# Two-layer hybrid encoder in split fp32: the grouped queries' product moved ahead of the keys' and values', with a separate inverse square root for the keys

## The chip, the cores and the metric

The kernel runs on one core of one Trainium2 chip, as one program. The metric is the device time of one execution in microseconds (us). A core has a matmul engine (PE), whose weight loads (PEld) overlap its matmuls, and three engines for elementwise work: DVE, ACT and POOL. SP issues the DMAs. Matmuls write to PSUM, in banks of 128 partitions x 512 fp32 values; everything else lives in SBUF.

## The reference, cut to what matters

Input x is 512 tokens by 1024 channels in fp32. There are two layers. Each runs three branches over the same normalized input, merges them with gates, and ends with a gated MLP. The change touches the first product and the grouped-query branch.

```
h = rms_norm(x, attn_norm_g[l])
proj = h @ w_in[l]
c_q, c_kv, k_rope, gq, gk, gv, pool_in, gate_logits = split_columns(proj, IN_SIZES)
                 # 256,  128, 32, 512, 128, 128, 512, 3 x 1024 columns
def gqa_branch(q_raw, k_raw, v_raw, qn_g, kn_g, cos, sin):
    q = q_raw.reshape(b, s, GQA_HEADS, GQA_HEAD_DIM)       # 8 heads of 64
    k = k_raw.reshape(b, s, GQA_KV_HEADS, GQA_HEAD_DIM)    # 2 heads of 64
    v = v_raw.reshape(b, s, GQA_KV_HEADS, GQA_HEAD_DIM)
    q = apply_rope(rms_norm(q, qn_g), cos, sin)
    k = apply_rope(rms_norm(k, kn_g), cos, sin)
    o = block_attention(q, k, v)
o_mla  = mla_branch(c_q, c_kv, k_rope, ...)   # latents, own head norms and rope
o_pool = pool_branch(pool_in, ...)            # means over windows 2/4/8/16, minus the token
merged = sum over branches of sigmoid(gate) * (o_branch @ w_branch)
x = x + merged @ w_out[l]
x = x + (silu(u_gate) * u_val) @ ffn_w_down[l]   # u: conv of rms_norm(x) @ ffn_w_up
```

`rms_norm` divides by the root of the mean square over the last axis; for a head that is one number per token and head.

## The kernel before

**Split products.** Every fp32 operand of a matmul is held as a high and a low half (fp32r). A product (`mm3`) is three matmuls: high x high, high x low, low x high. The normalized input lies in `HH` and `HL`, channels on the partitions, in 8 chunks (`kc`). Its division by the root of the mean square (`rt`, or `rbc` spread over the partitions) is applied when a product is read out of PSUM.

**Weights.** All weights stream through SP's queue in the order in which they are used, into three buffers of up to 1024 columns (`raw`; the first eight pieces have buffers of their own). Two pieces before its use, a piece is split: ACT writes the high half `wh` (L209), then POOL, or DVE where a cost rule says so, the low half `wl` (L216). Each has four buffers. Lines L209 to L240 are those of a small wrapper class, `Engine`, which every operation of DVE, ACT and POOL goes through. So the profile names them by tile, and nearly all of an engine's work stands on a few lines.

**The order of the work.** It is not found at run time. The Python program that builds the kernel carries a model clock (`Clock`). Matmuls advance it. Elementwise work is put in as chains of steps: `chain(a, b, c)` puts `a` into a heap at its due time, and each next step is due when the model says that the one before is done. Steps come out in the order of their due times, and that is the order of the instructions on each engine; each engine then takes its instructions strictly in order. Steps of different chains interleave. Everything inside one step is issued without a break. `done(key)` and `need(key)` connect chains with the matmul stream, `at(t, fn)` puts in a single step at a time.

**PSUM.** Eight banks under five names: acc 2, S 1, ST 2, AV 2, mi 1. `ps(tag)` takes the next buffer of that name; on the chip its first matmul waits until the last reader of the buffer's former content is done.

**A layer's first part, in the order of PE.**

1. Latents (256 + 128 columns), token-major: 8 chunks x 4 token blocks x 3 matmuls, banks acc, acc, ST, ST. Then the sums for `rt` into S. On DVE `rsqrt_steps` computes an inverse square root in ten small operations: a first guess `y` from the bits (L228), then three rounds of three (`yt`, `yt`, `y`). Each of the ten is a step of its own, so others can come between. Then ACT copies the latents out (`lat_evac`, tile `mx`), their mean squares (`ssc`) go through the same ten steps, and `lat_norm` scales `mx` in eight DVE operations.
2. Four groups of pool channels, 8 x 3 matmuls each, banks AV, AV, mi, S. Each is read out by DVE (`pp`, times `rbc`), summed over its window in one to four additions (`win`), corrected at the edges and mixed (`mix`), and split (`mxh` on ACT, `mxl` on DVE).
3. Transposes of `mx` (L345), three banks: acc, acc, ST. They are split into `cth` (ACT) and `ctl` (DVE).
4. Keys, values and the rotary key of the latent branch, 288 columns, token-major, 96 matmuls, banks ST, AV, AV, mi. ACT copies each block out (`gkn`, values, `krt`), DVE forms the values' low halves, the sums of squares of the keys, and their rotary embedding in 16 operations (`gk_rope`).
5. Queries, 512 columns, 96 matmuls, banks acc, acc, ST, S; between chunks 3 and 4 the 12 matmuls of the pool product (`pool_product`), banks AV, AV, mi, ST. `gq_evac` copies each block out on ACT, its square's row sums are formed on DVE (`ssr`), and its rotary embedding runs on POOL and DVE (`gqr`).
6. One inverse square root for all 40 numbers per token block column, 32 of the queries and 8 of the keys (`rsqrt_steps(ssr, 40, ...)`), then the scaling of the keys (`gk`, done key `gkn`), then that of the four query blocks.
7. Gate products of the pool branch as a filler, `Filler`, in units of three matmuls: `PRE_A` = 13 units, and more while the planner's clock says that the keys are not ready. Then the keys' transposes, `gk_turn` (L345, bank mi, split into `ka` and `kb`), then the attention of the grouped queries, each step of it placed between filler units at a written position, then the latent branch in the same manner, whose heads use `rsqrt_steps` twice more (32 numbers each).

**The rotary tables** (`tables`, 12 DVE operations: constants times the head norms' gains, tiles `tabg`, `tabm`) come at planner time 28.0 in layer 0, and 8 us into layer 1.

Of the kernel before, what the change touches and what calls it, by code (L numbers as in the profile page):

```python
# [11 lines left out]
F32R = mybir.dt.float32r  # L12
I32 = mybir.dt.int32
# [60 lines left out]

def _widths():

    r = [384] * KC + [T] * 8 + [288] * KC + [T] * 4 + [T] + [T] * 4
    for br in (2, 1, 0):
        for k, _ in _order(br):
            r += WIDTHS[k]  # L80
    return r + [T] * (2 * KC) + [T] * (4 * FC) + [T] * (2 * FC)
# [36 lines left out]
class Clock:  # L118
# [37 lines left out]
    def done(self, *key):  # L156
        self.ready[key] = self.fin + self.SEM
# [86 lines left out]
def trunk(ctx: ExitStack, tc: tile.TileContext, x, w, prm, gb, cst, out):  # L244
# [41 lines left out]
    def f(ap):  # L286
        return ap.bitcast(F32)
# [118 lines left out]
    def rsqrt_steps(a, n, key):  # L406

        y = small("y0", [P, 64])[:, :n]
        t = small("yt", [P, 64])[:, :n]

        def newton(to):
            return [lambda: V.tensor_tensor(t, y, a, ALU.mult),
                    lambda: V.scalar_tensor_tensor(t, t, -0.5, y, ALU.mult, ALU.mult),
                    lambda: V.scalar_tensor_tensor(to, t, 1.5, y, ALU.add, ALU.mult)]

        return [lambda: V.tensor_scalar(y.bitcast(I32), a.bitcast(I32), -0.5, RSQRT_BITS, ALU.mult, ALU.add),
                *newton(y), *newton(y), *newton(a), lambda: done(*key)]

    def norm_finish(gen, sq, out):

# [45 lines left out]
    def rope_steps(dst, src, cs, sn, shape, half, eng2):  # L466

        hold = []

        def parts():  # L470
            t2 = slot("rp2")
            n = 1
            for s in shape[1:]:
                n *= s
            t2v = t2[:, :n].rearrange("p (a b) -> p a b", b=shape[-1])
            hold.append(t2v)
            eng2.tensor_tensor(t2v[:, :, 0:half], src[:, :, half:2 * half], sn[:, :, 0:half], ALU.mult)
            eng2.tensor_tensor(t2v[:, :, half:2 * half], src[:, :, 0:half], sn[:, :, half:2 * half], ALU.mult)
            if dst is not src:
                V.tensor_tensor(dst, src, cs, ALU.mult)  # L480

        def add():
            if dst is src:
                V.tensor_tensor(dst, src, cs, ALU.mult)
            V.tensor_tensor(dst, dst, hold[0], ALU.add)

        return [parts, add]

    def layer(l, sq, xsrc):
# [161 lines left out]
        kvb = [ps(t) for t in ktags]  # L651
        tok_major(kvb, 288)
        gkn, kj, gk1 = slot("gkn"), slot("kj"), slot("gk1")
        krt = small("krt", [P, 4, 32], bufs=1)
        VG = []
        for b in range(4):
            v = slot("vg", F32R)
            vh = v[:, 0:256].rearrange("p (h f) -> p h f", f=P)
            vl = v[:, 256:384].rearrange("p (h f) -> p h f", f=64)
            V.memset(f(vh[:, :, 64:P]), 1.0)  # L660
            VG.append((vh, vl))

        def kv_evac(b):
            vh, vl = VG[b]
            src = kvb[b][:, P:2 * P].rearrange("p (h f) -> p h f", f=64)
            A.activation(gkn[:, b * P:b * P + P], kvb[b][:, 0:P], AF.Copy, scale=rtok(b))
            A.activation(vh[:, :, 0:64], src, AF.Copy, scale=rtok(b))
            A.activation(krt[:, b, :], kvb[b][:, 2 * P:288], AF.Copy, scale=rtok(b))

            def lo():  # L670
                V.scalar_tensor_tensor(vl, src, rtok(b), f(vh[:, :, 0:64]), ALU.mult, ALU.subtract)
                free(ktags[b])
                done("vg", l, b)
            chain(lo, after=ck.fin - ck.now + 0.1)

        def gk_rope():
            for b in range(4):
                k = gkn[:, b * P:b * P + P].rearrange("p (h f) -> p h f", f=64)
                o = gk1[:, b * P:b * P + P].rearrange("p (h f) -> p h f", f=64)
                cs = bc(tabs[1][:, None, 64 * b:64 * b + 64], [P, 2, 64])  # L680
                sn = bc(tabs[1][:, None, 256 + 64 * b:320 + 64 * b], [P, 2, 64])
                for fn in rope_steps(o, k, cs, sn, [P, 2, 64], 32, V):
                    fn()

        def gk_sum():
            A.activation(kj[:, :T], gkn[:, :T], AF.Square)

        def gk_sum2():
            V.tensor_reduce(ssr[:, 32:40], kj[:, :T].rearrange("p (h f) -> p h f", f=64), AX.X, ALU.add)

        chain(*[lambda b=b: kv_evac(b) for b in range(4)], gk_sum, gk_sum2, gk_rope)

        opool = {}

        def pool_product():
            wh, wl = wnext()
            for g, tag in enumerate(("AV", "AV", "mi", "ST")):
                need(("mix", l, g))
                acc = ps(tag)
                ws = slice(g * P, g * P + P)  # L700
                mm3(acc, wh[:, ws], wl[:, ws], mixed[g][0][:, :T], mixed[g][1][:, :T], True, True)
                oh, ol = slot("oph", F32R), slot("opl", F32R)
                opool[g] = (oh, ol)
                chain(*split(oh[:, :T], ol[:, :T], acc, col(PRM_PS + g)),
                      lambda g=g, tag=tag: (free(tag), done("op", l, g)))


        qtags = ("acc", "acc", "ST", "S")
        gqb = [ps(t) for t in qtags]
        tok_major(gqb, T, pool_product)  # L710
        gqn = [slot("gq") for _ in range(4)]
        gqo = [slot("gqr") for _ in range(4)]

# [17 lines left out]
            chain(*rope_steps(o, q, cs, sn, [P, 8, 64], 32, G), lambda: done("gqr", l, b), after=dt - 0.4)  # L731

        def gq_mean():
            V.tensor_scalar(ssr, ssr, 1.0 / 64, EPS, ALU.mult, ALU.add)

        def gk_norm():
            o = gk1[:, :T].rearrange("p (h f) -> p h f", f=64)
            V.tensor_tensor(o, o, bc(ssr[:, 32:40].unsqueeze(2), [P, 8, 64]), ALU.mult)
            done("gkn", l)

        def gq_norm(b):
            o = gqo[b][:, :T].rearrange("p (h f) -> p h f", f=64)
# [1 line left out]
            done("gqn", l, b)  # L744

        chain(*[lambda b=b: gq_evac(b) for b in range(4)], ([("gqs", l, b) for b in range(4)], gq_mean),
              *rsqrt_steps(ssr, 40, ("ssr", l)), gk_norm,
              *[([("gqr", l, b)], lambda b=b: gq_norm(b)) for b in range(4)])

        KAB = []  # L750

# [637 lines left out]
def _pack_weights(i):  # L1389
    res = []  # L1390
    for l in range(L):
        cq, ckv, kr, gq, gk, gv, pool, gate = np.split(
            i["w_in"][l], np.cumsum([256, 128, 32, 512, 128, 128, 512]), axis=1)

        def rows(*parts):
            wm = np.concatenate(parts, axis=1)
            return [wm[kc * P:kc * P + P] for kc in range(KC)]

        res += rows(cq, ckv)
        for g in range(4):  # L1400
            res += _cut(_blocks(pool[:, g * P:g * P + P], KC))
        res += rows(gk, gv, kr)
        res += rows(gq)
# [103 lines left out]
```

## Time and profile before

| | |
|---|---|
| median of the runs | 1699.12 us (three runs, 1698.81 to 1700.99) |
| the profiled execution | 1701.64 us, of which the span of the core's instructions is 1699.4 |
| mean granted PE clock | 0.994 of full speed |
| busy share of the span | PE 97%, PEld 79%, POOL 57%, DVE 55%, ACT 46% |
| instructions in the span | 20370, of these PE 7360 matmuls, DVE 1502, ACT 1375, POOL 771 |
| DMA | 145.40 MB, 86 GB/s over the span |

The profile is that of one execution. Times in its views are in us from the start of the span; the chain of waits and the timeline name an instruction by engine, line (L341 is `mm`, L345 is `turn`), the tiles written and read (`out<-in`), and, in square brackets, how long the engine had stood idle before it and what released it. "<-DVE mx L228" says that an instruction of DVE on tile `mx`, line 228, ended that wait. A row of the timeline groups neighbours of the same form: the first number is its start, the second its length, x8 the count. A row of the windows view has, for a stretch of the span, its length, the busy time (and count) of PE, PEld, DVE, ACT and POOL, the granted PE clock, the DMA share, and the GB/s.

### The profile page before, as it was taken

What the parts mean: (1) busy time and instruction counts of PE and PEld (TensorE: products, weight loads), DVE (VectorE), ACT (ScalarE), POOL (GpSimd) and SP (SyncE); (2) the same over time, 40 slices, a digit from 0 to 9 for tenths busy, and PEclk for the clock granted to TensorE, in tenths of its full rate; (3) what the DMA queues carried; (4) which work ended last, traced back from release to release, by engine and by line L of the source; (5) the groups of instructions that cost most, each with busy time, mean ns of one, the idle gap of its engine ahead of it and who ended that gap; (6) DMA issues with size and microseconds to landing.
All of it is one profiled execution on the core that took longest, in us unless ns stands there. A gap on an engine that the chain in (4) does not pass through costs nothing.

```text
span 1699.4 us, 20370 instructions
## 1 busy us (share of the span) xinstructions
PE 1655.1 (97%) x7360; PEld 1335.7 (79%) x7360; DVE 938.3 (55%) x1502; ACT 782.6 (46%) x1375; POOL 972.3 (57%) x771
## 2 busy tenths in 40 slices
PE   8889999999999999999999899999999999999999
PEld 7767767778888888888888677777788888888887
DVE  6765976643356666630156759766433666666100
ACT  5356655653344444433234576556534444444221
POOL 4455565764566566655545565666645665666543
PEclk9999999999999999999999999999999999999999
DMA  5221112113423332333333211111233232232331
GB/s 176 85 72 44 56 48 62 38 62 112 124 87 89 98 100 87 100 106 116 100 101 95 70 44 47 61 49 38 75 118 118 87 100 92 94 94 93 111 118 56
DMA packets 44596, 145.40 MB, mean 86 GB/s; under 512 B 5072, under 2 KB 6352, under 8 KB 44496
## 3 DMA queue, kind: packets, MB, share of 16 engines
q1 hardware_dynamic: 44352, 144.10, 27.0%
q8 instruction: 58, 0.95, 0.2%
q14 instruction: 42, 0.34, 0.1%
q10 hardware_dynamic: 144, 0.01, 0.0%
HBM read 139.90 MB, written 4.19 MB: 85 GB/s over the span
## 4 chain that ended last, share of the span: by engine, by line
PE 87%; DVE 8%; issue 2%; ACT 1%; POOL 1%; DMA 0%; SPq 0%; POOLq 0%; DVEq 0%; ACTq 0%
PE ps_acc L341 40%; PE ps_ST L341 23%; PE ps_AV L341 20%; PE ps_S L341 2%; DVE gqr L216 1%; PE ps_mi L345 1%; DVE yt L216 1%; DVE nm L224 1%; POOL wl L216 1%; PE ps_mi L341 1%; DVE MQ L216 1%; DVE yt L220 0%; DVE win L216 0%; DVE y L220 0%; DVE y L228 0%
## 5 line engine op out<-in xcount | busy, mean ns | idle before, releaser
L216 POOL TENSOR_TENSOR wl<-raw,wh 128x512 fp32r<-128x512 f32 (+1 forms) x514 | 678.5, 1330 | 493.4 <-ACT wh L209 432.1
L209 ACT ACTIVATE wh<-raw 128x512 fp32r<-128x512 f32 (+3 forms) x522 | 313.8, 608 | 194.2 <-PE ps_ST L341 70.8
L220 DVE SCALAR_TENSOR_TENSOR a<-u,prm,a 128x512 f32<-128x512 f32 x176 | 239.6, 1362 | 79.2 <-ACT a L209 74.0
L341 PE MATMUL ps_acc<-HH,wh 128*128 128x512 f32 x624 | 247.1, 396 | 2.2 <-DVE XM L220 2.2
L341 PE MATMUL ps_acc<-HH,wl 128*128 128x512 f32 x624 | 246.7, 395 | 1.2 <-POOL wl L216 1.2
L341 PE MATMUL ps_acc<-HL,wh 128*128 128x512 f32 x624 | 246.2, 395 | 0.0
L216 POOL TENSOR_TENSOR pl<-pe,ph 128x512 fp32r<-128x512 f32 x105 | 138.9, 1325 | 110.4 <-ACT ph L209 70.4
L341 PEld LDWEIGHTS ps_acc<-HH,wh 128*128 128x128 f32 x624 | 117.5, 188 | 30.8 <-ACT mns L209 2.1
L341 PEld LDWEIGHTS ps_acc<-HH,wl 128*128 128x128 f32 x624 | 117.3, 188 | 30.0 <-POOL wl L216 2.5
L341 PEld LDWEIGHTS ps_acc<-HL,wh 128*128 128x128 f32 x624 | 117.5, 188 | 26.8
L209 ACT ACTIVATE pe<-ps_ST 128x512 f32<-128x512 f32 x128 | 76.3, 596 | 101.8 <-PE ps_ST L341 100.4
L224 DVE TENSOR_REDUCE nm<-ps_S 128x1 fp32r<-128x512 f32 x128 | 87.8, 686 | 57.3 <-PE ps_S L341 57.0
L216 POOL TENSOR_TENSOR al<-a,ah 128x512 fp32r<-128x512 f32 x44 | 58.1, 1320 | 84.8 <-ACT ah L209 56.5
L341 PE MATMUL ps_AV<-HH,wh 128*128 128x512 f32 x256 | 101.3, 396 | 0.0
L341 PE MATMUL ps_AV<-HH,wl 128*128 128x512 f32 x256 | 101.2, 395 | 0.0
L341 PE MATMUL ps_AV<-HL,wh 128*128 128x512 f32 x256 | 101.1, 395 | 0.0
L341 PE MATMUL ps_ST<-HH,wh 128*128 128x512 f32 x240 | 95.0, 396 | 0.0
L341 PE MATMUL ps_ST<-HH,wl 128*128 128x512 f32 x240 | 94.8, 395 | 0.0
L341 PE MATMUL ps_ST<-HL,wh 128*128 128x512 f32 x240 | 94.8, 395 | 0.0
L209 ACT ACTIVATE a<-u,prm 128x512 f32<-128x512 f32 x88 | 71.8, 816 | 32.4 <-DVE u L216 32.4
L209 ACT ACTIVATE ah<-a 128x512 fp32r<-128x512 f32 x44 | 27.8, 632 | 116.2 <-DVE u L240 110.8
L209 ACT ACTIVATE a<-a 128x512 f32<-128x512 f32 x44 | 27.8, 633 | 113.5 <-DVE u L240 113.5
(332 smaller groups left out, 3563.3 us busy)
## 6 DMA issues: line engine op xcount, KB each, us to landing
raw<-w SPq DMA_DIRECT2D x229, 512.0 KB, 3.5
raw<-w SPq DMA_DIRECT2D x13, 384.0 KB, 3.0
XM<-x SPq DMA_DIRECT2D x16, 256.0 KB, 3.8
raw<-w SPq DMA_DIRECT2D x6, 448.0 KB, 3.4
xsp<-XM SPq DMA_DIRECT2D x8, 256.0 KB, 2.0
XM<-xsp SPq DMA_DIRECT2D x8, 256.0 KB, 3.2
out<-XM SPq DMA_DIRECT2D x8, 256.0 KB, 2.5
raw<-w SPq DMA_DIRECT2D x4, 432.0 KB, 3.2
```

What stands on the lines that cost most here:

```text
L209: return self.eng.activation(out, in_, func, **k)
L216: return self.eng.tensor_tensor(out, *a)
L220: return self.eng.scalar_tensor_tensor(out, *a)
L224: return self.eng.tensor_reduce(out, in_, *a, **k)
L341: PE.matmul(o, lhsT=lhsT, rhs=rhs, start=start, stop=stop)
L345: PE.transpose(o, src, ident)
```

## The change

The order of steps 4 and 5 is swapped, and what hangs on it:

- **Queries first.** The query product stands directly behind the transposes of the latents, in the same banks as before (acc, acc, ST, S). The key/value product follows, with banks mi, ST, AV, AV, and the pool product now stands between its chunks 3 and 4, with banks acc, acc, S, ST. The weights are packed in the new order.
- **Two roots.** The queries' root takes 32 numbers; the keys have one of 8 in a chain of their own. Their copy out of PSUM (`gk_evac`, four ACT copies) comes before that of the values, and their rotary embedding is one run of four operations on a four-dimensional view instead of four runs on a block each.
- **One run of operations.** `rsqrt_steps` issues its ten operations in one step, everywhere.
- **Tables.** In layer 0 they come as soon as the last weight piece of the latents, the last `HL` and the last square are done; in layer 1 as before.

The filler's `PRE_A` = 13 and the loop that waits for `gkn` stay.

```diff
-    r = [384] * KC + [T] * 8 + [288] * KC + [T] * 4 + [T] + [T] * 4
+    r = [384] * KC + [T] * 8 + [T] * KC + [288] * 4 + [T] + [288] * 4
...
         def newton(to):
-            return [lambda: V.tensor_tensor(t, y, a, ALU.mult),
-                    lambda: V.scalar_tensor_tensor(t, t, -0.5, y, ALU.mult, ALU.mult),
-                    lambda: V.scalar_tensor_tensor(to, t, 1.5, y, ALU.add, ALU.mult)]
-
-        return [lambda: V.tensor_scalar(y.bitcast(I32), a.bitcast(I32), -0.5, RSQRT_BITS, ALU.mult, ALU.add),
-                *newton(y), *newton(y), *newton(a), lambda: done(*key)]
+            V.tensor_tensor(t, y, a, ALU.mult)
+            V.scalar_tensor_tensor(t, t, -0.5, y, ALU.mult, ALU.mult)
+            V.scalar_tensor_tensor(to, t, 1.5, y, ALU.add, ALU.mult)
+
+        def go():
+            V.tensor_scalar(y.bitcast(I32), a.bitcast(I32), -0.5, RSQRT_BITS, ALU.mult, ALU.add)
+            for to in (y, y, a):
+                newton(to)
+
+        return [go, lambda: done(*key)]
...
-        at(8.0 if l else 28.0, tables)
+        if l:
+            at(8.0, tables)
+        else:
+            chain(([("w", KC - 1), ("H", G1, KC - 1), ("sq", G1, KC - 1)], tables), after=16.0)
...
+        qtags = ("acc", "acc", "ST", "S")
+        gqb = [ps(t) for t in qtags]
+        tok_major(gqb, T)
...
+        def gq_mean():
+            V.tensor_scalar(ssr[:, 0:32], ssr[:, 0:32], 1.0 / 64, EPS, ALU.mult, ALU.add)
...
+        chain(*[lambda b=b: gq_evac(b) for b in range(4)], ([("gqs", l, b) for b in range(4)], gq_mean),
+              *rsqrt_steps(ssr[:, 0:32], 32, ("ssr", l)),
+              *[([("gqr", l, b)], lambda b=b: gq_norm(b)) for b in range(4)])
...
+            for g, tag in enumerate(("acc", "acc", "S", "ST")):        # pool_product
...
-        ktags = ("ST", "AV", "AV", "mi")
+        ktags = ("mi", "ST", "AV", "AV")
         kvb = [ps(t) for t in ktags]
-        tok_major(kvb, 288)
+        tok_major(kvb, 288, pool_product)
...
+        def gk_evac():
+            for b in range(4):
+                A.activation(gkn[:, b * P:b * P + P], kvb[b][:, 0:P], AF.Copy, scale=rtok(b))
+            chain(*rope_steps(heads(gk1), heads(gkn), *(
+                bc(tabs[1][:, o:o + 256].rearrange("p (b f) -> p b f", b=4)[:, :, None, :], [P, 4, 2, 64])
+                for o in (0, 256)), [P, 4, 2, 64], 32, V), lambda: done("gkr", l), after=ck.fin - ck.now)
...
+        def gk_square():
+            A.activation(kj[:, :T], gkn[:, :T], AF.Square)
+
+        def gk_sum():
+            V.tensor_reduce(ssr[:, 32:40], kj[:, :T].rearrange("p (h f) -> p h f", f=64), AX.X, ALU.add)
+            V.tensor_scalar(ssr[:, 32:40], ssr[:, 32:40], 1.0 / 64, EPS, ALU.mult, ALU.add)
...
-        chain(*[lambda b=b: kv_evac(b) for b in range(4)], gk_sum, gk_sum2, gk_rope)
...
-            for g, tag in enumerate(("AV", "AV", "mi", "ST")):         # pool_product
...
-        qtags = ("acc", "acc", "ST", "S")
-        gqb = [ps(t) for t in qtags]
-        tok_major(gqb, T, pool_product)
...
-        chain(*[lambda b=b: gq_evac(b) for b in range(4)], ([("gqs", l, b) for b in range(4)], gq_mean),
-              *rsqrt_steps(ssr, 40, ("ssr", l)), gk_norm,
-              *[([("gqr", l, b)], lambda b=b: gq_norm(b)) for b in range(4)])
+        chain(gk_evac, gk_square, gk_sum, *rsqrt_steps(ssr[:, 32:40], 8, ("ssk", l)), ([("gkr", l)], gk_norm))
+        chain(*[lambda b=b: kv_evac(b) for b in range(4)], after=2.0)
```

More of the change, by code (lines that the diff above doesn't have):

```diff
@@ L474, in parts @@
                 n *= s
-            t2v = t2[:, :n].rearrange("p (a b) -> p a b", b=shape[-1])
+            lead = {3: "p (a b) -> p a b", 4: "p (c a b) -> p c a b"}[len(shape)]
+            t2v = t2[:, :n].rearrange(lead, **dict(zip("ba" if len(shape) == 4 else "b", (shape[-1], shape[-2]))))
             hold.append(t2v)
-            eng2.tensor_tensor(t2v[:, :, 0:half], src[:, :, half:2 * half], sn[:, :, 0:half], ALU.mult)
-            eng2.tensor_tensor(t2v[:, :, half:2 * half], src[:, :, 0:half], sn[:, :, half:2 * half], ALU.mult)
+            one, two = (Ellipsis, slice(0, half)), (Ellipsis, slice(half, 2 * half))
+            eng2.tensor_tensor(t2v[one], src[two], sn[one], ALU.mult)
+            eng2.tensor_tensor(t2v[two], src[one], sn[two], ALU.mult)
             if dst is not src:
@@ L647, in layer @@
                   lambda j=j: (free(ctags[j]), done("latT", l, j)))
-        ktags = ("ST", "AV", "AV", "mi")
-        kvb = [ps(t) for t in ktags]
-        tok_major(kvb, 288)
[L653 to L686, printed above, removed]
@@ L688, in gk_sum2 @@
-        def gk_sum2():
-            V.tensor_reduce(ssr[:, 32:40], kj[:, :T].rearrange("p (h f) -> p h f", f=64), AX.X, ALU.add)
-        chain(*[lambda b=b: kv_evac(b) for b in range(4)], gk_sum, gk_sum2, gk_rope)
-        opool = {}
-        def pool_product():
-            wh, wl = wnext()
-            for g, tag in enumerate(("AV", "AV", "mi", "ST")):
[L698 to L705, printed above, removed]
@@ L733, in gq_mean @@
         def gq_mean():
[L734 to L739, printed above, removed]
+            V.tensor_scalar(ssr[:, 0:32], ssr[:, 0:32], 1.0 / 64, EPS, ALU.mult, ALU.add)
         def gq_norm(b):
@@ L746, in layer, with pool_product @@
         chain(*[lambda b=b: gq_evac(b) for b in range(4)], ([("gqs", l, b) for b in range(4)], gq_mean),
-              *rsqrt_steps(ssr, 40, ("ssr", l)), gk_norm,
+              *rsqrt_steps(ssr[:, 0:32], 32, ("ssr", l)),
               *[([("gqr", l, b)], lambda b=b: gq_norm(b)) for b in range(4)])
+        opool = {}
+        def pool_product():
+            wh, wl = wnext()
+            for g, tag in enumerate(("acc", "acc", "S", "ST")):
+                need(("mix", l, g))
+                acc = ps(tag)
+                ws = slice(g * P, g * P + P)
+                mm3(acc, wh[:, ws], wl[:, ws], mixed[g][0][:, :T], mixed[g][1][:, :T], True, True)
+                oh, ol = slot("oph", F32R), slot("opl", F32R)
+                opool[g] = (oh, ol)
+                chain(*split(oh[:, :T], ol[:, :T], acc, col(PRM_PS + g)),
+                      lambda g=g, tag=tag: (free(tag), done("op", l, g)))
@@ new lines, in layer @@
+        ktags = ("mi", "ST", "AV", "AV")
+        kvb = [ps(t) for t in ktags]
+        tok_major(kvb, 288, pool_product)
+        gkn, kj, gk1 = slot("gkn"), slot("kj"), slot("gk1")
+        krt = small("krt", [P, 4, 32], bufs=1)
+        VG = []
+        for b in range(4):
+            v = slot("vg", F32R)
+            vh = v[:, 0:256].rearrange("p (h f) -> p h f", f=P)
+            vl = v[:, 256:384].rearrange("p (h f) -> p h f", f=64)
+            V.memset(f(vh[:, :, 64:P]), 1.0)
+            VG.append((vh, vl))
@@ new lines, in gk_evac, with heads @@
+        def gk_evac():
+            for b in range(4):
+                A.activation(gkn[:, b * P:b * P + P], kvb[b][:, 0:P], AF.Copy, scale=rtok(b))
+            chain(*rope_steps(heads(gk1), heads(gkn), *(
+                bc(tabs[1][:, o:o + 256].rearrange("p (b f) -> p b f", b=4)[:, :, None, :], [P, 4, 2, 64])
+                for o in (0, 256)), [P, 4, 2, 64], 32, V), lambda: done("gkr", l), after=ck.fin - ck.now)
+        def heads(t):
+            return t[:, :T].rearrange("p (b h f) -> p b h f", b=4, h=2)
@@ new lines, in gk_square, with gk_norm @@
+        def gk_square():
[3 more added lines that the diff above has]
+            V.tensor_scalar(ssr[:, 32:40], ssr[:, 32:40], 1.0 / 64, EPS, ALU.mult, ALU.add)
+        def gk_norm():
+            o = gk1[:, :T].rearrange("p (h f) -> p h f", f=64)
+            V.tensor_tensor(o, o, bc(ssr[:, 32:40].unsqueeze(2), [P, 8, 64]), ALU.mult)
+            done("gkn", l)
@@ new lines, in kv_evac, with lo @@
+        def kv_evac(b):
+            vh, vl = VG[b]
+            src = kvb[b][:, P:2 * P].rearrange("p (h f) -> p h f", f=64)
+            A.activation(vh[:, :, 0:64], src, AF.Copy, scale=rtok(b))
+            A.activation(krt[:, b, :], kvb[b][:, 2 * P:288], AF.Copy, scale=rtok(b))
+            def lo():
+                V.scalar_tensor_tensor(vl, src, rtok(b), f(vh[:, :, 0:64]), ALU.mult, ALU.subtract)
+                free(ktags[b])
+                done("vg", l, b)
+            chain(lo, after=ck.fin - ck.now + 0.1)
@@ L1401, in _pack_weights @@
             res += _cut(_blocks(pool[:, g * P:g * P + P], KC))
+        res += rows(gq)
         res += rows(gk, gv, kr)
-        res += rows(gq)
         res.insert(len(res) - 4, i["pool_w"][l].transpose(1, 0, 2).reshape(P, T))
```

## The prediction

> **What bounds the kernel now.** I read the page's first part, then the list of who waited for whom on the matmul engine (engine, line, releaser: total us, times, longest us).
>
> ```profile
> PE 1655.1 (97%) x7360; PEld 1335.7 (79%) x7360; DVE 938.3 (55%) x1502; ACT 782.6 (46%) x1375; POOL 972.3 (57%) x771
> PE ps_S L341 <- DVE nm L224: 8.4, 7, 2.7
> PE ps_mi L345 <- DVE gk L216: 7.5, 2, 3.8
> PE ps_acc L345 <- DVE mx L228: 4.3, 1, 4.3
> 372.34 73.94 PE ps_acc L341 x318
> ```
>
> PE is busy for 97% of the span, and the change neither adds nor removes a matmul. What it can move is the remaining idle time, and the largest waits of PE are all on DVE. The last row, from the chain that ended last, prices a 512-wide matmul: 73.94/318 = 0.2325 us. A moved stretch of matmuls costs nothing by itself; what counts is whether its operands and its PSUM banks are ready.
>
> Next I read PE's timeline around the edited code (start, duration, idle time before it in brackets), and the clock in two stretches behind a long wait.
>
> ```profile
> 55.78 2.71 PE L345 MATMUL ps_acc<-C,mx 128*128 128x128 f32 x8 [4.31 <-DVE mx L228]
> 58.99 0.59 PE L341 MATMUL ps_ST<-wh,HH 128*128 128x288 f32 x1
> 114.09 0.66 PE L345 MATMUL ps_mi<-C,gk 128*128 128x128 f32 x4 [3.74 <-DVE gk L216]
> 119.66 0.51 PE L341 MATMUL ps_acc<-HH,wl 128*128 128x512 f32 x1 [0.44 <-POOL wl L216]
> 120.52 0.63 PE L345 MATMUL ps_mi<-C,gqr 128*128 128x128 f32 x4 [0.35 <-DVE kb L216]
> 123.85 0.44 PE L341 MATMUL ps_acc<-wh,cth 128*128 128x384 f32 x1 [0.95 <-ACT mqs L209]
> 895.79 1.03 PE L345 MATMUL ps_acc<-C,mx 128*128 128x128 f32 x8
> 897.02 0.38 PE L341 MATMUL ps_ST<-wh,HH 128*128 128x288 f32 x1
> 900.18 0.29 PE L341 MATMUL ps_mi<-wh,HL 128*128 128x288 f32 x1
> 901.45 0.40 PE L341 MATMUL ps_ST<-wh,HH 128*128 128x288 f32 x1 [0.98 <-ACT wh L209]
> 902.33 0.40 PE L341 MATMUL ps_ST<-wl,HH 128*128 128x288 f32 x1 [0.48 <-POOL wl L216]
> 909.36 0.41 PE L341 MATMUL ps_ST<-wl,HH 128*128 128x288 f32 x1 [0.37 <-POOL wl L216]
> 114.00:119.00 5.00, 4.91 (x18) 4.15 (x18) 4.28 (x8) 4.25 (x8) 0.68 (x1) 0.66 0.04 18
> 189.30:193.00 3.70, 3.70 (x10) 2.94 (x11) 3.67 (x8) 1.75 (x3) 0.00 (x0) 0.60 0.40 142
> ```
>
> To be seen: the transposes of the latents come at 55.78 (layer 0, after a wait) and at 895.79 (layer 1, without one), and the key/value product follows them with no wait of its own (58.99, 897.02). Later the turn of the keys waits 3.74 us in layer 0, and by the list as long in layer 1. After such a wait the granted clock (third number from the end in the last two rows) is 0.66 over 5 us: 5 x 0.34 = 1.7 us lost besides, called 1.5 below. The 24 matmuls from 897.02 to 900.18 price a 288-wide one at 3.16/23 = 0.137.
>
> **Query product first.** The queries' banks are acc, acc, ST, S; the keys' were ST, AV, AV, mi. The two acc banks are those in which the latents have just been turned. So the first query matmul waits until ACT's cth and DVE's ctl have read the first of them, and the second group waits for the second ctl; the key product, on other banks, waited for neither. The order of the built program agrees: both matmuls carry a wait on DVE, and ctl stands on DVE behind three of the four pool groups and the evacuation of the fourth. Nothing on PE can pass them. So DVE's lateness at ctl, which cost nothing so far, becomes the price.
>
> ```profile
> 883.71 1.27 DVE L228 TENSOR_SCALAR y<-ssc 128x8 int32<-128x8 int32 x1
> 885.21 1.16 DVE L220 SCALAR_TENSOR_TENSOR yt<-yt,y 128x8 f32<-128x8 f32 x1
> 886.41 1.21 DVE L220 SCALAR_TENSOR_TENSOR y<-yt,y 128x8 f32<-128x8 f32 x1
> 883.16 4.44 POOL L216 TENSOR_TENSOR wl<-raw,wh 128x512 fp32r<-128x512 f32 x3 [1.01 <-ACT wh L209]
> 891.37 0.17 DVE L220 SCALAR_TENSOR_TENSOR yt<-yt,y 128x8 f32<-128x8 f32 x1
> 55.38 1.92 DVE L228 TENSOR_SCALAR mx<-mx,ssc 128x256 f32<-128x256 f32 x8
> 891.29 0.63 ACT L209 ACTIVATE mxh<-win 128x512 fp32r<-128x512 f32 x1 [5.79 <-DVE win L220]
> 896.09 0.70 DVE L216 TENSOR_TENSOR win<-pp 128x518 f32<-128x518 f32 x1
> 901.17 1.41 DVE L220 SCALAR_TENSOR_TENSOR ctl<-ps_acc,prm,cth 128x512 fp32r<-128x512 f32 x2
> ```
>
> Layer 1 on DVE. Up to 887.6 (four of the ten operations of the root) nothing differs. Then, by the new order: six operations at 0.2 to 888.8; mxl 0.6; eight scalings 1.92 to 891.3; pool group 1 (evacuation 0.6, two windows 1.3, edges 0.3, mix 0.6) to 894.1; its mxh on ACT (0.63 and two semaphores, together 0.8), which DVE now waits out because no other chain stands between, and mxl 0.65 to 895.6; group 2's evacuation 0.65 and three windows of 0.7, of which two meet the first query splits on POOL (0.5 each), to 899.4; edges and mix to 900.3; mxh and mxl 1.4; the last group's evacuation 0.65; ctl 0.7: 903.05. Query matmuls start at 903.2, not at 897.02: **+6.2**. The second ctl comes a window (0.65) and a ctl (0.7) later while PE has 0.7 of work: **+0.6**. The clock after the wait: **+1.5**. The three key waits (0.98 + 0.48 + 0.37, in layer 1 alone) end because query pieces are used at 2.8 us each: **-1.8**. Layer 1: **+6.5**. Bounds: +3 (no collisions, the clock kept) to +9 (every window stuck).
>
> What is a collision? The y, yt, y of 883.71 to 887.6 took 1.2 us each, not 0.17: each lasted until POOL's split of that moment ended. The Trainium skill (SBUF — State Buffer, "Who interferes with whom") states it as an exclusive lock, held for a whole instruction, between GpSimd and a DVE instruction with two SBUF inputs or in a two-port mode; the trace agrees (1.16 against 0.17). By that rule a run of ten tiny operations in one go wins little against a busy POOL. With that lock the walk of layer 0 below would end at its later bound, without it at its earlier one, 2.0 us apart.
>
> **Layer 0, with the tables moved.**
>
> ```profile
> 38.98 3.62 DVE L216 TENSOR_TENSOR tabg<-C,gb 128x256 f32<-128x256 f32 x4
> 38.84 2.80 POOL L216 TENSOR_TENSOR wl<-raw,wh 128x512 fp32r<-128x512 f32 x2 [1.00 <-ACT wh L209]
> 22.00 2.12 DVE L216 TENSOR_TENSOR wl<-raw,wh 128x384 fp32r<-128x384 f32 x2
> 25.23 5.03 POOL L216 TENSOR_TENSOR wl<-raw,wh 128x512 fp32r<-128x512 f32 x4
> 28.56 0.17 DVE L228 TENSOR_SCALAR rt<-ps_S 128x8 f32<-128x8 f32 x1 [4.44 <-PE ps_S L341]
> 36.97 0.69 DVE L216 TENSOR_TENSOR pp<-ps_AV,rbc 128x512 f32<-128x512 f32 x1 [3.32 <-ACT rbc L209]
> ```
>
> The twelve table operations leave 38.5 to 43.3 and go into DVE's idle 4.44 us before rt, at 24.12. They would fit nearly (4.9 us), but POOL splits without a pause there, and an operation gets through once per split, as tabg did at 38.98. With three splits left before 29.0 (the fourth now follows the first evacuation on ACT) the tables end at about 31.6, rt runs 3 us later, its root meets no split (0.9 saved), and the root reaches the first pool evacuation some 2.5 us after 36.97, at 39.5; without collisions at 37.5. From there to ctl's end it is the same walk as in layer 1, 903.05 - 881.3 = 21.7 with its collisions: 59.2 to 61.2. Query matmuls start at 59.3 to 61.3 plus 0.6 for the second bank; the key product started at 58.99. So the 4.31 wait for mx goes, and a wait for ctl stands in its place, with the same cold clock: +0.9 to +2.9, **+2.0** taken. Bounds -2 to +4.
>
> **The keys' turn.** Now the keys come last, with a root of their own; the turn stands 13 units (39 matmuls, 9.1 us) behind the key product instead of 54 matmuls behind the query product.
>
> ```profile
> 97.04 0.69 DVE L224 TENSOR_REDUCE ssr<-gqs 128x8 f32<-128x512 f32 x1
> 106.64 1.29 DVE L216 TENSOR_TENSOR gqr<-gqr,rp 128x512 f32<-128x512 f32 x1
> 110.04 1.52 DVE L216 TENSOR_TENSOR gqr<-gqr,rp 128x512 f32<-128x512 f32 x1
> 113.34 0.69 DVE L216 TENSOR_TENSOR gk<-gk,ssr 128x512 f32<-128x512 f32 x1
> ```
>
> Count from the end of the query product. PE reaches the turn after 96 x 0.137 (12.8 to 13.1), 12 x 0.2325 and 39 x 0.2325: 25.0. On DVE all query work stands first. Here it ended at 111.5, 13.9 after that product's end (97.6, that is 114.09 - 3.74 - 54 x 0.2325 with the rounding of the last matmul). There it shares POOL with the key splits as it shared it here with gate splits (additions 1.29 and 1.52, not 0.6), gains one split of its own (0.8) and two scaled pool splits (1.4), and loses a gate product and the root's first steps (2.8): about 15. Then two more pool splits 1.4, the root 2.1 to 3.5, four scalings 2.5, memsets 0.6, and one collision: 22 to 24. Only then the keys: rope 2.0 (four operations for sixteen), sum 0.6, mean 0.2, value halves 1.2, root 2.1, scaling 0.7: 29 to 31. PE waits 4 to 6, **5.0** taken, against 3.74: +1.3 a layer. Behind it the three waits of 0.44, 0.35 and 0.95 shrink to about 0.5, since the query heads are long ready: -1.2. Both layers together **+0.2**; bounds -8 (no wait at all) to +6.
>
> Key splits: POOL holds the query rope (8 us) and splits in 15.6 us; by its order each piece is ready a microsecond ahead: 0, bounds 0 to +3. The two roots of the latent heads now run in one go, so a row maximum (nm) queued behind them comes up to three small operations later, 0.2 each or 1.2 in a collision, and PE's single S bank waits for it: **+1**, bounds -3 to +5 (of the 8.4 us listed above).
>
> **Sum.** +6.5 + 2.0 + 0.2 + 1 = +9.7. The profiled execution took 1701.64 us (span 1699.4); it is 2.5 above the median of the runs, 1699.12. I forecast 1711.3 for a profiled one and **1708.8** for the median.
>
> **Rivals.** (1) DVE keeps up: ctl is done as the transposes end. Then layer 1 gives -1.8, layer 0 -5 (4.31 and what the cold clock added), the rest +1.2: 1693.5. It decides where DVE reaches ctl before 897.5. For it: the tables leave the stretch, and ten tiny operations no longer alternate with windows; against: in this profile ctl starts at 901.17, with less standing before it. Chance 0.10. (2) The keys' root is in time, as its separation suggests: -7.5 for both turns, -2.4 behind them, -3 of clock, with +6.5 + 2.0 + 1 in front: 1695.7. It decides where DVE ends the query work by 18 rather than 23 us after the product. Chance 0.12. (3) Waits only change places, each new one taking up what an old one had left: layer 1's +6.5 is paid back within the slack of the following turn: about 1700, chance 0.10. The forecast keeps 0.68.
>
> **Range.** The forecast's own bounds, taken halfway as they hardly fall together, are 1701 to 1719; the range reaches to rival 2's place below, 1695, and 1720 above. A measurement of this kernel can tell about 0.2%, 3.4 us, from no change. Faster: both first rivals, less a fifth that ends within it: 0.17. Within 0.2%: 0.12. Slower: 0.71.
>
> **What would show it.** Right: in both layers the first 512-wide matmul into acc behind the transposes waits for DVE ctl, some 6 us in layer 1; the 4.31 for mx is gone; gk still holds PE for 4 to 6 us; the three waits on key splits at 901 to 909 are gone. Wrong: no wait on ctl, no wait on gk, or new waits on wl during the key product.

## The result, and the profile after

The changed kernel took 1716.01 us (median of four runs, 1714.36 to 1717.88), the kernel before, measured beside it, 1700.05 (1698.81 to 1702.38). The ratio is 1.0091, with a 95% interval of 1.0078 to 1.0105: 16 us slower. Forecast were 1708.8, or 9.7 slower: the direction was right, and 6 to 7 us were missing. The profiled execution took 1717.88 us, its span is 1716.1, 16.7 above that of before.

First the page's line of engines, then the list of who waited for whom (engine, tile and line, releaser: us in total, times, longest):

```profile
PE 1661.0 (97%) x7360; PEld 1344.0 (78%) x7360; DVE 952.5 (56%) x1513; ACT 777.3 (45%) x1361; POOL 977.0 (57%) x772
...
PE ps_acc L341 <- DVE ctl L220: 13.7, 2, 7.7
PE ps_S L341 <- DVE nm L224: 12.7, 8, 3.5
PE ps_mi L345 <- DVE gk L216: 9.4, 2, 4.7
```

The wait for `mx` (4.3 before) is gone, and the two waits on `ctl` that were forecast stand at the head of the list. `gk` rose from 7.5 to 9.4. The second line is the surprise: the waits for `nm`, the row maxima of the attention, rose from 8.4 to 12.7, where about 1 more had been forecast. The three waits on weight pieces in layer 1's key product (0.98, 0.48, 0.37) are gone, as forecast.

The place of the first wait, in PE's timeline, and the granted clock (third number from the end) in the windows behind it:

```profile
50.78 1.03 PE L345 MATMUL ps_acc<-C,mx 128*128 128x128 f32 x8
51.65 0.60 PE L345 MATMUL ps_ST<-C,mx 128*128 128x128 f32 x4
59.94 0.79 PE L341 MATMUL ps_acc<-wh,HH 128*128 128x512 f32 x1 [7.69 <-DVE ctl L220]
...
910.73 0.79 PE L341 MATMUL ps_acc<-wh,HH 128*128 128x512 f32 x1 [6.03 <-DVE ctl L220]
```

```profile
60.00:65.00 5.00, 5.00 (x12) 3.78 (x13) 4.90 (x7) 0.65 (x2) 2.67 (x2) 0.50 0.23 60
911.00:916.00 5.00, 5.00 (x13) 3.74 (x14) 4.87 (x8) 0.44 (x1) 2.67 (x2) 0.53 0.31 82
```

In layer 0 the transposes come 5.0 us earlier than before (50.78 against 55.78), and the product behind them 0.95 later (59.94 against 58.99). In layer 1 the transposes come 7.45 later (903.24 against 895.79), the product 13.71 later: 6.3 us lost in that gap alone.

For a balance, PE's timeline of both kernels was cut at the same matmuls. Between the end of the query, key and value products and the first transposes of the latent heads the two orders differ by 3 matmuls (0.7 us) that stand on the other side of the first query turn; the table counts them on one side.

| stretch | before, us | after, us | change |
|---|---|---|---|
| layer 0: start to end of the q, k, v products | 4.85 to 97.55 | 4.93 to 100.72 | +3.1 |
| to the first turn of the query heads | to 120.52 | to 123.71 | +0.7 |
| grouped attention, to the first turn of the latent heads | to 255.19 | to 263.47 | +4.4 |
| rest of layer 0, to the transposes of layer 1 | to 895.79 | to 903.24 | -0.8 |
| layer 1: to the end of the q, k, v products | to 937.60 | to 951.14 | +6.1 |
| to the first turn of the query heads | to 960.87 | to 973.82 | +0.1 |
| grouped attention | to 1095.64 | to 1112.46 | +3.2 |
| rest | to 1695.18 | to 1711.87 | -0.1 |

### The profile page after: what moved, and what is told of

The parts are those of the page before. It is cut to its first block, busy times and chain, and to the rows that moved or that the text cites. A ratio compares the mean times of both kernels' runs of the same rounds, so it can differ in the third digit from the quotient of the medians.

```text
span 1716.1 us, 20372 instructions
## 1 busy us (share of the span) xinstructions
PE 1661.0 (97%) x7360; PEld 1344.0 (78%) x7360; DVE 952.5 (56%) x1513; ACT 777.3 (45%) x1361; POOL 977.0 (57%) x772
## 4 chain that ended last, share of the span: by engine, by line
PE 85%; DVE 12%; ACT 1%; issue 1%; DMA 1%; SPq 0%; DVEq 0%; ACTq 0%
PE ps_acc L341 40%; PE ps_ST L341 22%; PE ps_AV L341 18%; PE ps_S L341 2%; PE ps_mi L345 1%; DVE gqr L216 1%; DVE MQ L216 1%; DVE nm L224 1%; DVE win L216 1%; DVE yt L216 1%; DVE yt L220 1%; DVE y L220 1%; DVE pl L216 0%; DVE osum L236 0%; DVE wl L216 0%
## 5 line engine op out<-in xcount | busy, mean ns | idle before, releaser
L216 POOL TENSOR_TENSOR wl<-raw,wh 128x512 fp32r<-128x512 f32 (+3 forms) x512 | 677.9, 1333 | 508.1 <-ACT wh L209 450.6
```

Of the source, the lines that this page charges most:

```text
L216: return self.eng.tensor_tensor(out, *a)
```

## The experiments

Ratios are to the kernel before, run beside each on the same chip, with 95% intervals; 0.001 is 1.7 us. The intervals reach 0.0009 to 0.0014 to either side, so two ratios less than some 0.002 (3 us) apart cannot be told from each other. Profile rows are of one execution each: single waits and stretches can be read in them, while what a run costs in all is taken from the ratios.

### Other banks: does the query product wait only for its banks?

```diff
-ctags = ("acc", "acc", "ST")             +ctags = ("AV", "AV", "mi")      # latents' transposes
-qtags = ("acc", "acc", "ST", "S")        +qtags = ("acc", "acc", "ST", "ST")
-ktags = ("mi", "ST", "AV", "AV")         +ktags = ("S", "mi", "AV", "AV")
-("acc", "acc", "S", "ST")                +("acc", "acc", "ST", "ST")      # pool_product
```

> The changed kernel with the latents' transposes in banks AV, AV, mi, the queries in acc, acc, ST, ST, keys and values in S, mi, AV, AV and the pool product in acc, acc, ST, ST, so that no query matmul needs a bank that ctl has to free. Theory (the query product waits only because its first banks are those of the latents): both waits on ctl go (7.7 in layer 0, 6.0 in layer 1) and the slow clock behind them (2.7 and 2.3), some 17 to 19 us in all, so about 1698 from 1716; the wait of the keys' turn stays near 4.7 in each layer, since DVE stood idle for more than 9 us in the query product. Rival (DVE's lateness is only passed on): the turn's wait grows by what the ctl wait loses, up to 6 us in each layer, and the time stays above 1708.

1703.53 us, ratio 1.0007 (0.9997 to 1.0017), against 1.0091 of the change as made: 14 us back. In the list of waits `ctl` no longer appears, and `gk` stands where it stood:

```profile
PE ps_S L341 <- DVE nm L224: 12.7, 8, 3.5
PE ps_mi L345 <- DVE gk L216: 9.4, 2, 4.7
```

DVE itself did nothing sooner. Its timeline has the first `ctl` of layer 0 at 59.49, and the changed kernel's at 59.15; in layer 1 it starts 6.7 us behind the first transpose in both.

```profile
59.49 0.74 DVE L220 SCALAR_TENSOR_TENSOR ctl<-ps_AV,prm,cth 128x512 fp32r<-128x512 f32 x1
```

So the theory holds: `ctl` is as late as in the changed kernel, and nobody waits for it. The lateness is not passed on to the keys' turn. Of what was expected beyond 14 us, some 2 went to waits on weight pieces in the query product (0.61 and 0.85 us in layer 0, 0.86 in layer 1), which were absent as long as PE stood waiting.

### Roots as separate steps again

Two runs of the changed kernel: only the two roots of the latent heads (`ssmq`, `ssm`) as ten steps, and all of them.

```diff
+        if key[0] in ("ssmq", "ssm"):
+            return [*ops, lambda: done(*key)]
+        return [lambda: [op() for op in ops], lambda: done(*key)]
```

> The changed kernel with the two roots of the latent heads as ten separate steps again, the others in one run. Theory (a row maximum queued behind ten operations in one run holds the single S bank): the time lost in the grouped attention falls from 16.5 and 14.5 us to about 12 in each layer, nm waits from 8.4 and 7.2 to about 5.5; 1716 becomes about 1709. Rival (the maxima come late since the attention starts after 13 units of filler, not 18): nm waits stay and so does the time, 1716. The ctl and gk waits stay in either case.

> The changed kernel with all roots as separate steps again. Theory: as with the latent heads' roots alone, about 1709, and the ctl waits move by less than 1 us, since the same operations stand ahead of ctl on DVE. Rival (one run carries the latents' root past the busy POOL faster): the ctl waits grow by 2 us or more in each layer, so 1713 or above. Other rival (one run is what makes ctl and gk late): they shrink by 2 us or more, 1703 or less.

The first gave 1713.64 us, 1.0068 (1.0056 to 1.0080); the second 1712.63, 1.0058 (1.0046 to 1.0071). From 1.0091 that is 3.9 us for the latent heads' roots and 5.6 for all, less than the 7 that were expected; the two runs cannot be told from each other. The waits of the second, with all roots apart:

```profile
PE ps_acc L341 <- DVE ctl L220: 11.8, 2, 6.1
PE ps_mi L345 <- DVE gk L216: 8.8, 2, 4.4
PE ps_S L341 <- DVE nm L224: 6.9, 4, 3.9
PE ps_acc L341 <- ACT mns L209: 5.2, 2, 2.6
```

`nm` falls from 12.7 to 6.9, but some of it comes back as a wait on `mns`, the squares of the latent keys (2.1 in the changed kernel, 5.2 here). `ctl` shrinks by 1.9 in both layers together, and moves neither rival's way by the 2 us in each layer that it asked for.

How a run holds up a row maximum is seen in the changed kernel's DVE timeline, and below it in PE's:

```profile
187.30 0.69 DVE L224 TENSOR_REDUCE nm<-ps_S 128x1 fp32r<-128x512 f32 x1
187.90 0.85 DVE L228 TENSOR_SCALAR ssm<-ssm 128x32 f32<-128x32 f32 x1
188.79 0.67 DVE L228 TENSOR_SCALAR y<-ssm 128x32 int32<-128x32 int32 x1
...
189.94 1.25 DVE L220 SCALAR_TENSOR_TENSOR y<-yt,y 128x32 f32<-128x32 f32 x1
191.22 1.19 DVE L216 TENSOR_TENSOR yt<-y,ssm 128x32 f32<-128x32 f32 x1
...
193.46 0.68 DVE L224 TENSOR_REDUCE nm<-ps_S 128x1 fp32r<-128x512 f32 x1
```

```profile
188.95 0.39 PE L341 MATMUL ps_S<-ka,qa 128*128 128x512 f32 x1
...
194.19 0.50 PE L341 MATMUL ps_S<-ka,qa 128*128 128x512 f32 x1 [3.45 <-DVE nm L224]
```

The scores are there at 189.3. Their maximum is queued behind the rest of the run, starts at 193.46, and the next scores need the same single bank.

### One run alone, in the kernel before

> The kernel before with every root in one run and nothing else changed. Theory (the run holds up the row maxima whatever the order of the products): the nm waits of the grouped attention grow from 5.4 to about 8 us in each layer, with some 1.5 of slow clock; in front, the latents' root is done sooner, so the wait of 4.3 for mx in layer 0 and the slow clock behind it (2.5) shrink or go; together 0 to +5, about 1703. Rival (one run matters only together with the new order): nm waits stay near 5.4, and the time falls to 1695 by the wait for mx.

1707.46 us, 1.0035 (1.0022 to 1.0047): 6 us slower with nothing changed but how ten operations are issued. The waits:

```profile
PE ps_S L341 <- DVE nm L224: 13.0, 6, 4.3
PE ps_mi L345 <- DVE gk L216: 9.9, 2, 5.0
```

`nm` goes from 8.4 to 13.0 in the old order, `gk` from 7.5 to 9.9, and the wait for `mx` vanishes as expected: the run carries the latents' root past the pool windows. Most of that gain is used up by waits on weight pieces behind it (`ACT wh` into ST, 4.5 us where 1.0 stood before). The cost of the run is therefore shown by itself, and it does not need the new order.

### The tables

The changed kernel with the tables of layer 0 at 28.0 again, and the kernel before with them moved.

> The changed kernel with the tables of layer 0 at their old time. Theory (their twelve operations, 4.9 us on DVE, then stand in the stretch that ends with ctl): the wait on ctl in layer 0 grows from 7.7 by 2 to 4 us, so about 1719; layer 1 does not move. Rival (the tables only move the root rt, and ctl comes at the same time): within 1 us of 1716.

> The kernel before with the tables of layer 0 moved and nothing else changed. Theory (in the old order the only wait of PE in this stretch is that for mx, and twelve operations less stand ahead of it): the wait of 4.3 and the 2.5 of slow clock behind it go, layer 1 and the keys' turns do not move: about 1695. Rival (rt is held up by the tables and carries its lateness on): the wait for mx shrinks by 2 us or less, 1699 to 1701.

1716.67 us, 1.0080 (1.0067 to 1.0094), and 1702.62 us, 1.0005 (0.9995 to 1.0016). Neither moves the time by what can be told. My expectation for each was wrong; in the first the rival's time came about. Three rows of DVE's timeline, of the kernel with the tables at their old time:

```profile
29.64 0.17 DVE L228 TENSOR_SCALAR rt<-ps_S 128x8 f32<-128x8 f32 x1 [7.09 <-PE ps_S L341]
46.44 1.41 DVE L216 TENSOR_TENSOR tabg<-C,gb 128x256 f32<-128x256 f32 x4
59.81 0.74 DVE L220 SCALAR_TENSOR_TENSOR ctl<-ps_acc,prm,cth 128x512 fp32r<-128x512 f32 x1
```

and of the changed kernel:

```profile
23.35 5.79 DVE L216 TENSOR_TENSOR tabg<-C,gb 128x256 f32<-128x256 f32 x4
29.87 0.15 DVE L228 TENSOR_SCALAR rt<-ps_S 128x8 f32<-128x8 f32 x1
59.15 0.74 DVE L220 SCALAR_TENSOR_TENSOR ctl<-ps_acc,prm,cth 128x512 fp32r<-128x512 f32 x1
```

The four tables take 5.79 us where POOL works without a pause, 1.41 where it mostly rests. Moved, they end just as `rt` can start. Left at 28.0 they stand before `ctl`, yet push it by 0.66 only. While they run, two pool groups come due together, and DVE finds work of one while it would wait for `mxh` of the other (two waits of 0.69 us in the changed kernel, none here). POOL also has no split left when the next windows run (three for 2.06 us, not 3.40). In the kernel before, the wait for `mx` went as expected, and the key and value product started 5.5 us sooner (53.44, not 58.99). But in the profile of that run the product then took 41.47 us, not 38.56, with 2.7 more on weight pieces (`ACT wh` into ST 2.8 and `POOL wl` 1.7 in all, 1.0 and 0.8 before), and the attention of the two layers 2.0 us more. Its span is 1696.2 against 1699.4. It was the fastest of twelve executions, and the medians show no gain at all: why is open.

### The order alone

The changed kernel with both of these undone: what remains is the order and the keys' own root.

> The changed kernel with roots as separate steps and the tables at their old time: the new order of the products and the keys' own root remain. Theory (the parts add up): the ratio to before is 1.0091 less 1.0035 - 1 for the one run and 1.0005 - 1 for the tables, that is 1.005, some 1709 against 1700; ctl waits of about 6 us in both layers, nm waits as before. Rival (the parts are worse together than apart): 1.002 or less. Other rival (the order carries all of it): 1.008 or more.

1710.29 us, 1.0057 (1.0044 to 1.0071). The parts add up: 0.0057 for the order with the keys' own root, 0.0035 for the run, 0.0005 for the tables, 0.0097 against 0.0091 measured.

```profile
PE ps_mi L345 <- DVE gk L216: 8.8, 2, 4.4
PE ps_S L341 <- DVE nm L224: 7.0, 4, 4.0
PE ps_acc L341 <- DVE ctl L220: 6.2, 2, 5.6
PE ps_acc L345 <- DVE mx L228: 5.3, 1, 5.3
```

One point differs from what was expected: in layer 0 `ctl` holds PE for 0.6 us only, since PE has already waited 5.3 for `mx`. It is one lateness of DVE, paid at the first place where PE asks for it.

### The filler and the keys' turn

The changed kernel with `PRE_A` = 19; then the kernel before, in its old order, with separate roots for keys (8) and queries (32), without and with the tables moved.

> The changed kernel with 19 units of filler ahead of the keys' turn, not 13. Theory (the turn waits since the keys come 4.7 us late; the filler of the attention has room to spare): the wait on gk falls from 4.7 to below 1 in each layer, the slow clock behind it goes, and the attention loses 1 to 3 more on nm: 1708 to 1712. Rival (what DVE has to do up to the end of the attention sets the time, so the wait goes to the row maxima): within 2 us of 1716.

> The kernel before, in its old order, with a root of 8 for the keys right after their own product and a root of 32 for the queries; nothing else changed. Theory (in the old order the keys wait only for the root they share with the queries): the wait on gk (3.9 in each layer) and the slow clock behind it (1.6) go, the query turn or a row maximum takes back a third: 1692 to 1696 against 1700. Rival (DVE's work up to the first row maxima sets the time, whatever PE waits for): the wait moves to gqr, and the time stays within 2 us of before.

> The same with the tables of layer 0 moved as in the change. Theory: with the tables out of the way the wait for mx goes, but as the kernel before with the tables alone stood at 1.0005, within 2 us of the run without them. Rival (the tables bring the 7 us that the wait for mx and its slow clock cost): 5 us or more below it.

1714.11 us, 1.0076 (1.0062 to 1.0089) with 19 units: 2.5 us less, which is not clear of the noise. The theory's 1708 is out; its 1712 is not ruled out, nor is the rival's 1716. The wait on `gk` (9.4) is gone from its list, and this stands there:

```profile
PE ps_acc L341 <- DVE ctl L220: 12.9, 2, 6.9
PE ps_S L341 <- DVE nm L224: 12.3, 6, 4.2
PE ps_acc L341 <- ACT wh L209: 10.4, 5, 5.3
PE ps_acc L341 <- DVE gt L216: 6.4, 2, 3.2
```

`ACT wh` was 4.9 and `gt` was absent: PE now waits 5.5 us more for weight pieces and 6.4 for DVE to empty an acc bank of the filler, where 9.4 for the keys had stood. The waits for `nm` did not take it up.

1706.17 us, 1.0024 (1.0015 to 1.0033), with roots apart in the old order; 1703.47, 1.0010 (1.0001 to 1.0019), with the tables too, which is not clear of the run without them. The theory of the first fell: the keys are in time, and the kernel is 4 us slower. PE's timeline of the first of these two:

```profile
106.54 0.60 PE L345 MATMUL ps_mi<-C,gk 128*128 128x128 f32 x4
...
115.19 0.66 PE L341 MATMUL ps_acc<-wh,cth 128*128 128x384 f32 x1 [3.19 <-DVE gt L216]
...
120.22 0.77 PE L341 MATMUL ps_acc<-HH,wh 128*128 128x512 f32 x1 [2.77 <-DVE XM L220]
121.64 1.06 PE L345 MATMUL ps_mi<-C,gqr 128*128 128x128 f32 x4
```

The keys turn at 106.54 without a wait. But DVE is still in the queries' root (up to 113.1), and now the filler behind the turn asks for its acc banks, which DVE has to empty (`gt`, `XM`): 3.19 + 2.77 where 3.74 for `gk` had stood. The query turn comes at 121.64, before at 120.52.

### The two remedies together

The changed kernel with the other banks and all roots as separate steps.

> The changed kernel with the other banks (no query matmul waits for ctl) and all roots as separate steps. Theory (the two losses lie in different stretches and add up): the ratio to before is 1.0007 - (1.0091 - 1.0058) = 0.997, about 1696. Rival (they share DVE's lateness, so undoing one takes part of the other): 1.000 or above.

1697.81 us, 0.9979 (0.9969 to 0.9988): 1.1% below the change as made, and 0.2% below the kernel before. 0.0007 less 0.0033 had given 0.9974, so the two losses are separate. Together they are more than the 16 us measured: without them the change would have gained 3.6 us. What is left in its list:

```profile
PE ps_mi L345 <- DVE gk L216: 8.8, 2, 4.4
PE ps_S L341 <- DVE nm L224: 6.9, 4, 3.9
```

## Why the prediction was right, and where it was short

The wait, its place and its size in layer 1 were right; the attention, and in layer 0 the clock, were sized too small or left out.

**Query product first, layer 1: +6.5 forecast, +6.1 measured.** The wait is the one that was named, in the place that was named. The walk was counted as 21.7 us from the first pool evacuation to the end of `ctl`; it took 22.3, from 888.41 to 910.68:

```profile
888.41 0.69 DVE L216 TENSOR_TENSOR pp<-ps_AV,rbc 128x512 f32<-128x512 f32 x1 [4.03 <-ACT rbc L209]
...
902.19 0.69 DVE L216 TENSOR_TENSOR mxl<-win,mxh 128x512 fp32r<-128x512 f32 x1 [0.70 <-ACT mxh L209]
...
904.63 2.37 DVE L216 TENSOR_TENSOR win<-win 128x516 f32<-128x516 f32 x2
...
908.70 0.69 DVE L216 TENSOR_TENSOR mxl<-win,mxh 128x512 fp32r<-128x512 f32 x1 [0.69 <-ACT mxh L209]
909.34 0.68 DVE L216 TENSOR_TENSOR pp<-ps_S,rbc 128x512 f32<-128x512 f32 x1
909.94 0.74 DVE L220 SCALAR_TENSOR_TENSOR ctl<-ps_acc,prm,cth 128x512 fp32r<-128x512 f32 x1
```

Each step named is there: the waits for `mxh`, the windows stretched to 2.37 for two by the query splits, the last evacuation, `ctl`. The product starts 6.3 us later (+6.2 forecast). From its start to its end the three products take 40.4 us, 40.6 before, so the rest comes to -0.2 (+0.3 forecast). In it two terms were off and cancelled: the clock fell to 0.53, not 0.66 (2.3 us lost, 1.5 forecast), and the second bank cost nothing (+0.6 forecast), because the slow matmuls gave DVE time for the second `ctl`. That the sum came out is in part luck.

**Layer 0: +2.0 forecast, +3.1 measured.** `ctl` was put at 59.2 to 61.2, and ended at 59.9. The tables held `rt` up by far less than the 3 us forecast: it starts at 29.87, and at 29.64 with the tables at their old time. So the product starts only 0.95 us later, and here too the second bank cost nothing: less than half of the 2.0 forecast came about in that way. The step that failed is the clock, which the forecast let cancel ("with the same cold clock"). Before, most of the slow clock behind the wait for `mx` fell on the transposes: the product started 3.2 us after the first of them, against 1.2 in layer 1, so 2.0 us were already lost ahead of 58.99. Now all of it falls behind the start, and the three products take 40.8 us, 38.6 before: +2.2, where the forecast had nothing. The loss does not hang on the tables. With all roots apart the changed kernel stands at 1.0057 with the tables at their old time and at 1.0058 with them moved; in the first of these PE waits for `mx` in layer 0 instead.

**The keys' turn: +0.2 forecast for both layers, +0.8 measured.** The wait was put at 5.0 and is 4.7 in each layer. In the trace of the changed kernel all query work stands first on DVE, and the root of the keys, from 111.09 to 113.06, runs without a collision. The second rival, keys in time, fell with that. Keys in time would not have paid by themselves either: roots apart in the old order gave that, and nothing was won.

**The roots of the latent heads: +1 forecast, within -3 to +5; the attention lost 7.6.** This is the step that failed most: one term mis-sized, and one left out. The prediction let a row maximum come "up to three small operations later". With ten operations in one step nothing can come between, so it comes up to all ten later, and they take 4.4 us (228.18 to 232.56) to 5.5 (187.90 to 193.46) with their mean. The order, for its part, was given no cost in the attention at all. The profiles part the two; the stretches are those of the grouped attention, counted as in the table above:

| | layer 0, us | layer 1, us |
|---|---|---|
| before | 134.7 | 134.8 |
| new order, one run (the changed kernel, other banks, tables at 28.0) | 139.1 to 140.6 | 137.8 to 137.9 |
| new order, all roots apart (three runs) | 134.8 to 134.9 | 137.5 to 137.7 |

In layer 0 the run costs 4.2 to 5.8 us and the order next to nothing. In layer 1 the order costs 2.8 to 2.9 and the run less than 0.5. By the ratios the run costs 3.9 us for the latent heads' roots alone and 5.6 to 6.0 for all. In the order alone, PE waits 2.6 us for `mns` in each layer, where 0.6 had stood. In layer 0 the waits for `nm` fall by nearly as much (4.7 to 3.0). In layer 1 they rise (4.4 to 5.7), by a wait of 4.0 where 2.6 had stood. Its scores are there at 1031.6; this is DVE:

```profile
1030.17 1.32 DVE L216 TENSOR_TENSOR yt<-y,ssm 128x32 f32<-128x32 f32 x1
1031.53 1.21 DVE L220 SCALAR_TENSOR_TENSOR yt<-yt,y 128x32 f32<-128x32 f32 x1
...
1033.69 1.26 DVE L216 TENSOR_TENSOR yt<-y,ssm 128x32 f32<-128x32 f32 x1
1034.88 1.80 DVE L216 TENSOR_TENSOR pl<-pe,ph 128x512 fp32r<-128x512 f32 x1
...
1036.70 0.68 DVE L224 TENSOR_REDUCE nm<-ps_S 128x1 fp32r<-128x512 f32 x1
```

The separate steps met POOL's splits one after the other, and a split of DVE's own (`pl`) stood among them. That the new order brings these together is read from the rows and was not tested; why `mns` comes later was not examined.

**The rule of the lock.** The Trainium skill (SBUF — State Buffer, "Who interferes with whom") describes the SBUF ports that DVE shares with GpSimd as an exclusive lock, held for a whole instruction. In layer 1 the changed kernel's root of the latents has three operations of 1.17 to 1.27 us while POOL splits without a pause (890.28 to 894.74), and 0.17 from then on: the trace agrees. The prediction concluded that ten operations in one go win little. Here they won by going on where no split followed: the root ended 7.6 us after the first pool evacuation, in the kernel before 10.5. With the lock, layer 0's walk was to end at 61.2, without it at 59.2. The tables did collide (5.79 us), yet it ended at 59.9, since they were done about when `rt` could start.

**Rivals.** DVE did not keep up (first rival). Waits that only change places (third) are what the filler and the roots apart showed around the keys' turn; they are not what happened at `ctl`, where new banks brought 14 us and moved some 2 us of waits to weight pieces.

## What to carry to other kernels

When products change places, look at which PSUM banks the new neighbour takes over, and from whom: lateness of the reader that cost nothing can become a wait, and banks released earlier take it away without making any engine faster. A run of small operations on an engine that also serves a single-bank hand-over can delay that hand-over by the whole run, so leave gaps there. When a wait moves, ask also which matmuls now stand behind it and run slow. Where an engine is the one in arrears, being in time with one of its results only lets the next one wait.

## What was not expected of the hardware

The price of the slow clock did not follow from the length of the wait. Over the 5 us behind it the granted clock was 0.50 and 0.53 after 7.69 and 6.03 us in the changed kernel, but 0.68 after 5.68 with all roots apart. After the keys' turn in the run with other banks it was 0.50 in layer 0 (4.73 us) and 0.66 in layer 1 (4.65). A wait of 1.99 us in the changed kernel, at 1040.51, was followed by 0.66; one of 3.76 in the kernel before with the tables moved, at 111.46, by 1.00. So 0 to 2.5 us can be lost behind waits of similar length, and sums over single profiles carry that much chance.

Four table operations of 256 columns took 5.79 us beside POOL's work and 1.41 where POOL mostly rested.
